# A hybrid DeltaNet and attention block on one core: decay rows in three shared buffers, their exponents on ACT, the first modulation pairs ahead of the norm

## The chip, the cores and the metric

The kernel runs on one core of a Trainium2 chip. The metric is the device time of one execution in microseconds (us), lower is better. The engines are PE (matmuls, with weight loads shown as PEld), DVE (vector), ACT (scalar and activations), POOL (GpSimd) and SP (which issues DMAs). Each engine runs its instructions in the order of its own queue, and an instruction that waits holds up all that stand behind it on that engine.

## The reference

Two layers over 256 context and 256 latent tokens of width 2048. Layer 0 is a gated DeltaNet in chunks, run forward and backward; layer 1 is differential attention. Ahead of each layer the tokens are normed and modulated by shift and scale rows that come from `c` through `ada_w`. The part that the change touches most is the decay inside a chunk, cut to its core:

```python
gc = jnp.cumsum(chunks(g), axis=-1)
diff = gc[..., :, None] - gc[..., None, :]
decay = jnp.where(incl, jnp.exp(jnp.where(incl, diff, 0.0)), 0.0)
kb = kc * bc[..., None]
lower = jnp.where(strict, jnp.einsum('nbhid,nbhjd->nbhij', kb, kc) * decay, 0.0)
tinv = lax.linalg.triangular_solve(eye + lower, ...)
a_intra = jnp.einsum('nbhid,nbhjd->nbhij', qc, kc) * decay
```

## The kernel before

All 512 tokens stand along the free dimension, 128 channels of a head on the partitions. The program is written in Python; a scheduler with a timeline model of its own sorts the instructions of each engine, so that the order on an engine is not that of the code. The head of the program (`body`, lines 296 to 330) loads the tokens `xt`, sums their squares into `acc0`, makes the norm row `rrow0` with two matmuls into `iv`, and computes shift and scale pair by pair: `ada_load` brings the modulation weights `ar` on SP's queue, `ada_pair` multiplies them on PE into the PSUM banks `gq` or `tr` and puts the result into `shv` and `scv`. `make_h` then forms the modulated tokens `hhi` and `hlo` (a value and its rest), which three early projections `ba`, `k0`, `q0` use. `gates` makes the gate rows: the cumulated log decay goes to DRAM as `gc_d` and stays in SBUF as `gct` (with the log of beta taken in), `lnb` holds the limit.

The DeltaNet stage runs over 16 groups `g` of two heads, each with 4 chunks of 128 tokens and both directions. A small event loop (`Drive`) with written priorities sets the order in which the generators are written down: `stream_b` (the recurrence: tiles `yb`, `x`, `S`, `O`, with PSUM `sb` and `so`), `stream_lev` (the levels of the triangular inverse: `T`, `U`, `R`, `uf`, with PSUM `iv`), `stream_at` and `stream_m` (the matrices `at` and `ma`, with PSUM `gq`), `stream_ada` (later modulation, POOL and ACT in turn on `rp`), and `filler` (the projections of the next groups, PSUM `pj`: weights are loaded as raw pieces, cast to `hi` on ACT, the rest `lo` taken on POOL, three buffers each, six matmuls for each piece of 256 columns).

For each chunk, `stream_m` and `stream_at` call `decay` once: 64 times for tiles named `grm` and 64 times for `gra`. It loads four rows of `gc_d`, each copied to all 128 partitions, with two DMAs on SP's queue; makes four DVE instructions of 128x128 that subtract `gct` and take the minimum with `lnb`; and one ACT exponential over 128x512. `scaled` then multiplies the result with the masked Gram matrix `gm` on DVE (line 700) into `ma` or `at`, which frees the buffer. Each of the two tags has one buffer (line 683):

```python
gr = dl.tile([P, 4, P], F32, tag=tag, name=f"{tag}{g}{c}", bufs=1)
```

`block_inv` inverts the 16x16 blocks with a chain of small DVE products (`bP`, `bY`), casts the result into `TU` and stores it to DRAM (`tu_d`), from where `stream_lev` loads `T` and `U` on SP's queue. After the stage the output projections (`woA`, `woB`) and layer 1 follow; their tiles `yr`, `yl` and `woA0r` already appear at the end of the DeltaNet stage.

Of the kernel before, what the change touches and what calls it, by code (L numbers as in the profile page):

```python
# [10 lines left out]
F32 = mybir.dt.float32  # L11
F32R = mybir.dt.float32r
F16 = mybir.dt.float16
BF16 = mybir.dt.bfloat16
AF = mybir.ActivationFunctionType
ALU = mybir.AluOpType
# [4 lines left out]
P = 128  # L21
T = 512
NCH = 4
# [38 lines left out]
def body(ctx, tc, D, d, out):  # L62
    nc = tc.nc
    KT = D // P
    G = KT
    HV = 2 * KT
# [97 lines left out]
    def ada_load(l, pr, pl, tag, bufs):  # L164
        W = 8 * P
        for q in range(2 * D // W):
            r = pl.tile([P, W], F32, tag=tag, name=f"ar{l}_{pr}{q}", bufs=bufs)
            o = q * W % D
            nc.sync.dma_start(r, d["adaw"][l, 2 * pr + q * W // D, :, o:o + W])
            for k in range(W // 256):  # L170
                yield r[:, k * 256:(k + 1) * 256]

    def ada_pair(l, pr, rs, ps, pl):
        for kt, r in enumerate(rs):
            j = 32 * (kt % 4)
            mm(ps[j:j + 32, :256], sc2[:, kt, :], r, kt < 4, kt >= KT - 4)
        row = pl.tile([P, 256], F32, tag="arow", name=f"arow{l}_{pr}", bufs=1)
        nc.scalar.copy(row, ps[:, :256])
        for hf in range(2):
            mm(ps[:, 256 + 2 * hf:258 + 2 * hf], row[:, hf * P:(hf + 1) * P], sel4)  # L180
        for hf in range(2):
            ada_put(l, 2 * pr + hf, ps[:, 256 + 2 * hf:258 + 2 * hf], True)
# [67 lines left out]
    tr = lambda: pt_("tr", 1)  # L250
    iv = lambda: pt_("iv", 2)
# [7 lines left out]

    gp_cm = pool("gp", side="right")  # L260
    gp = gp_cm.__enter__()
    gct, eg, kd, egl, lnb = (gp.tile([P, NCH, 2, HV], F32, name=n) for n in ("gct", "eg", "kd", "egl", "lnb"))
    zt = gp.tile([P, P], F16, name="zt")
    nc.vector.memset(zt, 0.0)
    t0_cm = pool("t0", reuse_waits="tile")
# [1 line left out]
    HKT = KT // 2  # L267
# [27 lines left out]
    ta = ta_cm.__enter__()  # L295
    with tc.high_priority():
        for kt in range(KT):
            nc.sync.dma_start(xt[kt], d["xT"][:, kt])
        nc.scalar.activation(acc0, xt[0], AF.Square)
        for kt in range(1, KT):  # L300
            sq = ta.tile([P, T], F32, tag="mh", name=f"sq{kt}", bufs=2)
            nc.scalar.activation(sq, xt[kt], AF.Square)
            nc.vector.tensor_tensor(acc0, acc0, sq, ALU.add)
        nc.scalar.copy(rrow0, rstd_rows(acc0, T, iv, ta.tile([P, 4, P], F32, name="rr_dg0")))
        np_ = 0
        for k0 in range(0, KT, SK):
            for kind in range(2):
                pr = kind * HKT + k0 // 2
                ada_pair(0, pr, ada_load(0, pr, ta, "ar", 8), (gq, tr)[np_ % 2](), ta)
                np_ += 1  # L310
            for kt in range(k0, k0 + 2):
                make_h((xt[kt][:, 0:256], xt[kt][:, 256:512]), kt, rrow0, 0, hhi, hl, ta, nc.gpsimd)
            for n, src, _ in EARLY:
                w = SK * P
                r = ta.tile([P, w], F32, tag="er", name=f"e{n}r{k0}", bufs=6)
                nc.sync.dma_start(r, src[:, k0 * P:k0 * P + w])
                hi = ta.tile([P, w], F32R, tag="eh", name=f"e{n}h{k0}", bufs=6)
                lo = ta.tile([P, w], F32R, tag="el", name=f"e{n}l{k0}", bufs=6)
                split(hi, lo, r)
                for k in range(SK):  # L320
                    kt, ks = k0 + k, slice(k * P, (k + 1) * P)
                    ps = early[n]
                    mm(ps, hi[:, ks], hhi[:, kt, :], kt == 0, False)
                    mm(ps, hi[:, ks], hl(kt), False, False)
                    mm(ps, lo[:, ks], hhi[:, kt, :], False, kt == KT - 1)
        ta_cm.__exit__(None, None, None)
        convw = load_small("convw", [P, 4 * KT, 5], d["convw"], gp)
        adt = load_small("adt", [P, 2, 2, HV],
                         d["adt"].to_broadcast([P, NB]).rearrange("p (k d h) -> p k d h", k=2, d=2), gp)
# [31 lines left out]
    def gates(ps):  # L361
# [46 lines left out]
        def softplus(k):  # L408
            t, e, u, w = t2[k], tl(f"e{k}", sh), tl(f"u{k}", sh), tl(f"w{k}", sh)
            nc.scalar.activation(e, t, AF.Abs)  # L410
            nc.scalar.activation(e, e, AF.Exp, scale=-1.0)
            nc.vector.tensor_scalar(u, e, 2.0, None, ALU.add)
            nc.vector.reciprocal(w, u)
            nc.vector.tensor_tensor(u, e, w, ALU.mult)
            nc.vector.tensor_tensor(e, u, u, ALU.mult)
            nc.vector.tensor_scalar(w, e, 2.0 / 17.0, None, ALU.mult)
            for m in (15, 13, 11, 9, 7, 5, 3):
                nc.vector.scalar_tensor_tensor(fl(w), fl(w), 2.0 / m, fl(e), ALU.add, ALU.mult)
            nc.vector.scalar_tensor_tensor(fl(w), fl(w), 2.0, fl(u), ALU.add, ALU.mult)
            nc.vector.scalar_tensor_tensor(fl(w), fl(t), 0.0, fl(w), ALU.max, ALU.add)  # L420
            return w
# [3 lines left out]
        nc.vector.tensor_tensor(g, w, wide(ea), ALU.mult)  # L425
        tri = lambda dd: cs[:, C_TRI + dd * P:C_TRI + (dd + 1) * P]
        for a in range(2):
            p3 = (gq, tr)[a]()
            for c in range(2):
                for dd in range(2):  # L430
                    q = 2 * c + dd
                    mm(p3[:HV, q * P:(q + 1) * P], g[:, 2 * a + c, dd, :], tri(dd))
            r = tl(f"r{a}", [HV, 4, P])
            nc.scalar.copy(r.rearrange("p q i -> p (q i)"), p3[:HV])
            nc.sync.dma_start(gc_d[2 * a:2 * a + 2].rearrange("c (d h) i -> h (c d) i", d=2), r)
# [4 lines left out]
                mm(p1v[:, c, dd, :], tri(dd), g[:, c, dd, :])  # L440
        mm(p1[:, n:2 * n], ones, fl(g))
        nc.vector.tensor_scalar(t2[0], bt, -1.0, None, ALU.mult)
        nc.vector.tensor_scalar(lnb, softplus(0), -1.0, None, ALU.mult)
        tc.keep_in_program_order(nc.scalar.activation(eg, p1v, AF.Exp))
        tc.keep_in_program_order(nc.scalar.dma_start(sc_d.rearrange("s (p i) -> (s p) i", i=W2), rc))
        nc.scalar.activation(egl, p1[:, n:2 * n].rearrange("p (c d h) -> p c d h", c=NCH, d=2), AF.Exp)
        raw = tl("raw", sh)
        nc.vector.tensor_copy(raw, p1v)
        nc.vector.tensor_tensor(gct, raw, lnb, ALU.subtract)
        e = tl("be", sh)  # L450
        nc.scalar.activation(e, bt, AF.Exp, scale=-1.0)
        nc.vector.tensor_scalar(e, e, 1.0, None, ALU.add)
# [227 lines left out]
        return t.rearrange("p (u i) -> p u i", u=4)  # L680

    def decay(g, c, s, tag):
        gr = dl.tile([P, 4, P], F32, tag=tag, name=f"{tag}{g}{c}", bufs=1)
        gsrc = gc_d[c].rearrange("(d h) i -> d h i", d=2)
        for dd in range(2):
            nc.sync.dma_start(gr[:, 2 * dd:2 * dd + 2, :],
                              gsrc[dd:dd + 1, 2 * g:2 * g + 2, :].rearrange("d h i -> d (h i)").to_broadcast([P, 2 * P])
                              .rearrange("p (h i) -> p h i", h=2))
        for u in range(4):
            dd, h = divmod(u, 2)  # L690
            j = 2 * g + h
            nc.vector.tensor_scalar(gr[:, u], gr[:, u], gct[:, c, dd, j:j + 1], lnb[:, c, dd, j:j + 1],  # L692
                                    ALU.subtract, ALU.min)
        nc.scalar.activation(gr, gr, AF.Exp)  # L694
        return gr

    def scaled(o, gr, pg, s, nm):
# [5 lines left out]
    def block_inv(g, half, m16):  # L703
        par = half
        nm = f"{g}{half}"
        nc.scalar.dma_start(full(mb_d[par]), m16.rearrange("p d c h i -> p (d c h) i"))
        bk = dl.tile([64, 16, 16], F16, tag="bk", name=f"bk{nm}", bufs=1)
        nc.sync.dma_start(bk, diag(mb_d[par]))
        X = dl.tile([64, 16, 16], F32, tag="bX", name=f"bX{nm}", bufs=1)
        Y = dl.tile([64, 16, 16], F32, tag="bY", name=f"bY{nm}", bufs=1)  # L710
        pr = dl.tile([64, 16, 16], F32, tag="bP", name=f"bP{nm}", bufs=1)
        TU = dl.tile([64, 2, 16, 16], F16, tag="bT", name=f"bT{nm}", bufs=1)
        nc.vector.tensor_scalar(X[:32], bk[:32].rearrange("p j i -> p i j"), -1.0, None, ALU.mult)
        nc.vector.tensor_scalar(X[32:], bk[32:], -1.0, None, ALU.mult)
        nc.scalar.copy(Y, e16[:64])  # L715
        for i in range(1, 16):
            nc.vector.tensor_tensor(pr[:, :i, :i], X[:, i, :i].unsqueeze(1).to_broadcast([64, i, i]),  # L717
                                    Y[:, :i, :i].rearrange("p j c -> p c j"), ALU.mult)
            nc.vector.tensor_reduce(Y[:, i, :i], pr[:, :i, :i], AX.X, ALU.add)  # L719
        for dd in range(2):  # L720
            ps_ = slice(32 * dd, 32 * dd + 32)
            nc.scalar.copy(TU[ps_, dd], Y[ps_])
            nc.scalar.copy(TU[ps_, 1 - dd], Y[ps_].rearrange("p j i -> p i j"))
        for j in range(2):
            nc.scalar.dma_start(diag(tu_d[par][j]), TU[:, j])
        return [tu_d[par][j].rearrange("(d c h) (j i) -> c j d h i", d=2, c=2, i=P) for j in range(2)]
# [574 lines left out]
```

## Time and profile before

| | us |
|---|---|
| median of 3 runs (3129.51 to 3135.29) | 3134.51 |
| the profiled execution | 3130.73 |
| its span, first to last instruction | 3128.9 |
| PE busy (90% of the span) | 2817.8 |
| POOL busy (64%) | 2012.8 |
| DVE busy (63%) | 1955.8 |
| ACT busy (60%) | 1872.4 |

The mean granted clock of PE over the span is 0.963. The busy shares are means over stages of different kinds: head (to some 140 us), the start of the DeltaNet stage (to 300 us), its steady part (to 2000 us), output projections and layer 1. So they are read by stretch, then by who waits for whom within a stretch. Durations come from the profiled execution; 1.8 us of its time lie outside the span.

### The profile page before, as it was taken

To read this page: it belongs to the slowest core of one execution; us is meant where nothing else is said; L and a number is where in the kernel's file an instruction comes from. 1 tells how busy PE (TensorE), PEld (TensorE's weight loads), DVE (VectorE), ACT (ScalarE), POOL (GpSimd) and SP (SyncE) were. 2 spreads that over 40 slices of the span, in tenths; PEclk is the share of its full clock that TensorE was granted. 3 is DMA by queue.
4 is the path that set the end of the run, shared out by engine and by line. 5 is a ranking of instruction groups with operands and counts; after the bars stand their busy time and mean duration, and the time that the engine had idled before them with its cause. 6 is when DMAs were issued, how large, how long until landed. Compare 5 with 4: busy or idle time off the path is not lost. (4 is left out here: it accounts for less than half of the span.)

```text
span 3128.9 us, 52162 instructions
## 1 busy us (share of the span) xinstructions
PE 2817.8 (90%) x16178; PEld 2239.7 (72%) x16178; DVE 1955.8 (63%) x4287; ACT 1872.4 (60%) x5466; POOL 2012.8 (64%) x2370
## 2 busy tenths in 40 slices
PE   5788988988988988988898888899998999999998
PEld 2465767766766766766776666688687888888897
DVE  2178688688678677688578678632335654544454
ACT  4345766766766666766666666654556666654353
POOL 2366777777767777777777777466565666752334
PEclk8899999999999999999999999999999999999999
DMA  9646555456545545445456445667744555543345
GB/s 339 235 100 139 124 127 130 127 119 135 126 118 133 134 116 139 117 125 139 117 126 137 121 120 138 173 178 207 238 147 120 162 155 162 160 142 109 115 130 164
DMA packets 510312, 457.03 MB, mean 146 GB/s; under 512 B 241744, under 2 KB 380752, under 8 KB 510032
## 3 DMA queue, kind: packets, MB, share of 16 engines
q1 hardware_dynamic: 299456, 342.48, 37.7%
q10 hardware_dynamic: 210576, 111.22, 14.9%
q8 instruction: 127, 2.08, 0.3%
q14 instruction: 153, 1.25, 0.1%
HBM read 427.18 MB, written 26.36 MB: 145 GB/s over the span
## 5 line engine op out<-in xcount | busy, mean ns | idle before, releaser
L139 ACT ACTIVATE rp<-rp 128x256 f32<-128x256 f32 x1024 | 426.8, 417 | 298.2 <-POOL rp L138 292.6
L717 DVE TENSOR_TENSOR bP<-bX,bY 64x1 f32<-64x1 f32 (+14 forms) x480 | 225.1, 469 | 22.0 <-ACT bY L715 14.2
L139 ACT ACTIVATION_READ_ACCUMULATOR rp<-rp 128x1 f32 x1024 | 194.2, 190 | 0.0
L692 DVE TENSOR_SCALAR grm<-grm,gct,lnb 128x128 f32<-128x128 f32 x256 | 133.2, 563 | 84.8 <-DMA grm<-gc_d 84.1
L692 DVE TENSOR_SCALAR gra<-gra,gct,lnb 128x128 f32<-128x128 f32 x256 | 116.0, 493 | 85.0 <-DMA gra<-gc_d 84.7
L786 DVE TENSOR_TENSOR R<-iv,lv 128x512 f16<-128x512 f32 x192 | 127.1, 680 | 28.7 <-PE iv L83 28.5
L83 PEld LDWEIGHTS <-m 128*128 128x128 f16 x1024 | 76.2, 100 | 78.7 <-issue 71.5
L694 ACT ACTIVATE grm<-grm 128x512 f32<-128x512 f32 x64 | 40.3, 630 | 129.1 <-DVE grm L692 125.3
L719 DVE TENSOR_REDUCE bY<-bP 64x1 f32<-64x1 f32 (+14 forms) x480 | 108.6, 226 | 8.0
L750 POOL TENSOR_TENSOR ma<-ma,cs 128x512 f32<-128x512 f32 x64 | 86.5, 1352 | 32.3 <-DVE ma L700 30.0
L83 PE MATMUL iv<-T,m 128*128 128x128 f16 x768 | 74.3, 225 | 32.5 <-DMA T<-tu_d 19.1
L83 PE MATMUL iv<-U,R 128*128 128x128 f16 x768 | 76.9, 227 | 28.5 <-DVE R L786 26.4
L694 ACT ACTIVATE gra<-gra 128x512 f32<-128x512 f32 x64 | 40.4, 631 | 103.8 <-DVE gra L692 103.7
L83 PEld LDWEIGHTS <-R 128*128 128x128 f16 x768 | 48.8, 101 | 70.9 <-DVE R L786 37.9
L224 DVE TENSOR_TENSOR hlo<-mh,hhi 128x512 fp32r<-128x512 f32 x32 | 25.9, 833 | 114.9 <-ACT hhi L223 87.8
L83 PE MATMUL sb<-yb,uf 128*128 128x128 bf16 x512 | 55.5, 225 | 32.5 <-DVE yb L910 20.9
L803 ACT CAST T<-iv 128x512 f16<-128x512 f32 x128 | 74.1, 579 | 16.2 <-PE iv L83 12.5
L753 POOL TENSOR_TENSOR ml<-ma,m 128x512 bf16<-128x512 f32 x64 | 75.3, 1177 | 6.2 <-ACT m L752 5.3
L83 PEld LDWEIGHTS <-uf 128*128 128x128 f16 x512 | 36.2, 100 | 57.3 <-issue 52.1
L804 ACT CAST U<-iv 128x512 f16<-128x512 f32 x128 | 75.9, 593 | 0.0
L83 PE MATMUL so<-x,at 128*128 128x128 f32 x512 | 73.3, 280 | 0.3 <-DVE sz L966 0.3
L83 PEld LDWEIGHTS so<-x,at 128*128 128x128 f32 x512 | 67.2, 195 | 2.6 <-PE sb L83 0.4
(2767 smaller groups left out, 11393.0 us busy)
## 6 DMA issues: line engine op xcount, KB each, us to landing
aw<-in_adaw_dram ACTq DMA_DIRECT2D x512, 128.0 KB, 2.9
ar<-in_adaw_dram SPq DMA_DIRECT2D x64, 512.0 KB, 7.5
grm<-gc_d SPq DMA_DIRECT2D x128, 128.0 KB, 4.4
gra<-gc_d SPq DMA_DIRECT2D x128, 128.0 KB, 4.5
mb_d<-m ACTq DMA_DIRECT2D x32, 256.0 KB, 4.9
U<-tu_d SPq DMA_DIRECT2D x128, 64.0 KB, 2.9
T<-tu_d SPq DMA_DIRECT2D x128, 64.0 KB, 3.3
yd<-sz SPq DMA_DIRECT2D x32, 256.0 KB, 3.7
```

Source lines behind the costliest of these rows:

```text
L83: nc.tensor.matmul(o, l, r, start=start, stop=stop)
L139: nc.scalar.activation(pr, pr, AF.Copy, accum_out=acc[:, s, q:q + 1])
L224: nc.vector.tensor_tensor(hlo(kt), t, hhi[:, kt, :].bitcast(F32), ALU.subtract)
L692: nc.vector.tensor_scalar(gr[:, u], gr[:, u], gct[:, c, dd, j:j + 1], lnb[:, c, dd, j:j + 1], ALU.subtract, ALU.min)
L694: nc.scalar.activation(gr, gr, AF.Exp)
L717: nc.vector.tensor_tensor(pr[:, :i, :i], X[:, i, :i].unsqueeze(1).to_broadcast([64, i, i]), Y[:, :i, :i].rearrange("p j c -> p c j"), ALU. ...
L719: nc.vector.tensor_reduce(Y[:, i, :i], pr[:, :i, :i], AX.X, ALU.add)
L750: nc.gpsimd.tensor_tensor(ma, ma, ident.unsqueeze(1).to_broadcast([P, 4, P]), ALU.add)
L753: nc.gpsimd.tensor_tensor(ml[:, :, k], mv, m16[:, :, k], ALU.subtract)
L786: nc.vector.tensor_tensor(R, quad(pp), lvb(n), ALU.mult)
L803: nc.scalar.copy(Tm, quad(pt))
L804: nc.scalar.copy(U, quad(pu))
```

## The change

Four things are changed.

In the head, the loads of `xt` go in turn to SP's and ACT's queues; the two modulation pairs 0 and 8 (`HKT`) are written ahead of the norm and taken out of the loop's first turn.

`decay` has one tag of three buffers for `grm` and `gra`. The four DVE instructions become four ACT activations, Relu of (`gct` - row), and the exponential takes the negative of that; the limit is then zero and no longer `lnb`. `gates` keeps the softplus itself and adds it, so `lnb` falls away.

`TU` takes the buffer of `bP`. In `gates` the second transposed row block goes to `iv` in place of `tr`.

```diff
-    gct, eg, kd, egl, lnb = (gp.tile([P, NCH, 2, HV], F32, name=n) for n in ("gct", "eg", "kd", "egl", "lnb"))
+    gct, eg, kd, egl = (gp.tile([P, NCH, 2, HV], F32, name=n) for n in ("gct", "eg", "kd", "egl"))
...
         for kt in range(KT):
-            nc.sync.dma_start(xt[kt], d["xT"][:, kt])
+            (nc.sync, nc.scalar)[kt % 2].dma_start(xt[kt], d["xT"][:, kt])
+        for pr in (0, HKT):
+            ada_pair(0, pr, ada_load(0, pr, ta, "ar", 8), (gq, tr)[pr > 0](), ta)
         nc.scalar.activation(acc0, xt[0], AF.Square)
...
-            for kind in range(2):
+            for kind in range(2 if k0 else 0):
...
-            p3 = (gq, tr)[a]()
+            p3 = (gq, iv)[a]()
...
-        nc.vector.tensor_scalar(lnb, softplus(0), -1.0, None, ALU.mult)
+        nlnb = softplus(0)
...
-        nc.vector.tensor_tensor(gct, raw, lnb, ALU.subtract)
+        nc.vector.tensor_tensor(gct, raw, nlnb, ALU.add)
...
     def decay(g, c, s, tag):
-        gr = dl.tile([P, 4, P], F32, tag=tag, name=f"{tag}{g}{c}", bufs=1)
+        gr = dl.tile([P, 4, P], F32, tag="gr", name=f"{tag}{g}{c}", bufs=3)
...
-            nc.vector.tensor_scalar(gr[:, u], gr[:, u], gct[:, c, dd, j:j + 1], lnb[:, c, dd, j:j + 1],
-                                    ALU.subtract, ALU.min)
-        nc.scalar.activation(gr, gr, AF.Exp)
+            nc.scalar.activation(gr[:, u], gr[:, u], AF.Relu, scale=-1.0, bias=gct[:, c, dd, j:j + 1])
+        nc.scalar.activation(gr, gr, AF.Exp, scale=-1.0)
...
-        TU = dl.tile([64, 2, 16, 16], F16, tag="bT", name=f"bT{nm}", bufs=1)
+        TU = dl.tile([64, 2, 16, 16], F16, tag="bP", name=f"bT{nm}", bufs=1)
```

The scheduler sorts the engines anew. Three places show it.

SP's queue before, at the last two decays of the stage (`yr` and `woA0r` belong to the output projection; "x2" is two DMAs of one tile):

```order
L686 DMA gra_24410<-gc_d 128x256 x2
L119 DMA yr_24657<-yd 128x512
L119 DMA yr_24666<-yd 128x512
L119 DMA yr_24675<-yd 128x512
L119 DMA woA0r_24684<-in_wout_dram 128x512
L119 DMA yr_24690<-yd 128x512
L686 DMA gra_24422<-gc_d 128x256 x2
```

SP's queue after, at the same two decays (`g15z0r` and `g15z1r` are raw weights of the last projections):

```order
L778 DMA U_23485<-tu_d_89 128x2x128 x2
L778 DMA T_23484<-tu_d_88 128x2x128 x2
L778 DMA T_23490<-tu_d_88 128x2x128 x2
L778 DMA U_23491<-tu_d_89 128x2x128 x2
L119 DMA g15z0r_23819<-in_win_dram 128x512
L688 DMA gra_24408<-gc_d 128x256 x2
L688 DMA gra_24420<-gc_d 128x256 x2
L119 DMA g15z1r_23863<-in_win_dram 128x512
```

The two loads now stand next to each other, ahead of the last raw weights, and behind four loads of `U` and `T`.

DVE before, from the masked Gram matrix of that first decay to its product `at` (`yl` and `woA0lo` belong to the output projection):

```order
L699 TENSOR_TENSOR gm_24419<-gq,cs 128x256
L187 TENSOR_TENSOR yl_24636<-yr_24633,yh_24635 128x512
L187 TENSOR_TENSOR woA0lo_24645<-woA0r_24642,woA0hi_24644 128x512
L692 TENSOR_SCALAR gra_24410<-gra_24410,gct,lnb 128x128 x4
L910 TENSOR_TENSOR yb_24281<-v_23633,sb 128x512
L786 TENSOR_TENSOR R_24120<-iv,lv 128x512
L786 TENSOR_TENSOR R_24127<-iv,lv 128x512
L187 TENSOR_TENSOR yl_24651<-yr_24648,yh_24650 128x512
L187 TENSOR_TENSOR yl_24660<-yr_24657,yh_24659 128x512
L916 TENSOR_TENSOR x_24288<-x_24270,sb 128x512
L700 TENSOR_TENSOR at_24418<-gra_24410,gm_24419 128x512
```

DVE after, the same piece:

```order
L700 TENSOR_TENSOR gm_24417<-gq,cs 128x256
L187 TENSOR_TENSOR yl_24592<-yr_24589,yh_24591 128x512
L143 TENSOR_REDUCE am_16_26307<-al_16_26023 128x2
L911 TENSOR_TENSOR yb_24279<-v_23631,sb 128x512
L701 TENSOR_TENSOR at_24416<-gra_24408,gm_24417 128x512
```

ACT after, where the rows are now made (`g15z0hi` is a cast of a weight piece):

```order
L694 ACTIVATE gra_24408<-gra_24408,gct 128x128 x2
L185 CAST g15z0hi_23762<-g15z0r_23715 128x256
L694 ACTIVATE gra_24408<-gra_24408,gct 128x128 x2
L694 ACTIVATE gra_24420<-gra_24420,gct 128x128 x4
L904 CAST x_23732<-sb 128x512
L185 CAST g15z0hi_23774<-g15z0r_23772 128x256
L139 ACTIVATE rp_17_51_26218,al_17_26024<-rp_17_51_26218 128x256
L135 DMA aw_19_5_26229<-in_adaw_dram 128x256
L695 ACTIVATE gra_24408<-gra_24408 128x512
```

The four row instructions no longer stand ahead of `yb` and `R` on DVE; on ACT eight of them for two decays stand ahead of the cast `x` and the casts of weight pieces.

PE before, its first rows (`iv` from `cs` and `acc` sums the norm over channels, `iv` from `rr_dg` spreads it):

```order
L83 MATMUL iv<-cs,acc_130 128x1 x4
L83 MATMUL gq<-ar_00_228,sc_113 32x256 x4
L83 MATMUL gq<-ar_01_234,sc_113 32x256 x4
L83 MATMUL gq<-ar_02_240,sc_113 32x256 x4
L83 MATMUL iv<-rr_dg_213,cs 128x512
L83 MATMUL gq<-ar_03_246,sc_113 32x256 x4
```

PE after, its first rows:

```order
L83 MATMUL gq<-ar_00_167,sc_112 32x256 x4
L83 MATMUL gq<-ar_01_173,sc_112 32x256 x4
L83 MATMUL iv<-cs,acc_129 128x1 x4
L83 MATMUL gq<-ar_02_179,sc_112 32x256 x4
L83 MATMUL gq<-ar_03_185,sc_112 32x256 x4
L83 MATMUL tr<-ar_80_198,sc_112 32x256 x4
L83 MATMUL iv<-rr_dg_274,cs 128x512
```

Two groups of modulation matmuls moved ahead of the norm's first, and three ahead of its second.

## Rows read from the trace of the kernel before

**Rows 1.** Busy us of each engine by stretch, PE clock, DMA share, GB/s.

```profile
300.00:2000.00 1700.00, 1516.82 (x8975) 1179.18 (x8974) 1273.23 (x2978) 1123.44 (x3450) 1240.82 (x1546) 0.96 0.52 128
...
140.00:300.00 160.00, 126.18 (x567) 94.37 (x568) 122.09 (x252) 79.09 (x227) 95.02 (x113) 0.90 0.45 106
```

**Rows 2.** Waits of PE, 300 to 2000 us: total, times, longest, in us.

```profile
PE iv L83 <- DVE R L786: 26.5, 24, 3.3
PE sb L83 <- DVE yb L910: 18.2, 16, 3.3
...
PE iv L83 <- ACT T L803: 11.9, 12, 3.2
PE sb L83 <- ACT yb L884: 11.4, 10, 2.3
PE gq L83 <- DVE gm L699: 10.7, 8, 3.3
PE sb L83 <- DVE S L923: 9.5, 4, 3.8
PE sb L83 <- ACT x L903: 6.3, 7, 2.5
...
PE pj L83 <- ACT g4z0hi L185: 3.6, 1, 3.6
...
PE pj L83 <- ACT g9z0hi L185: 1.0, 1, 1.0
```

**Rows 3.** DVE's groups, 300 to 2000 us: busy, mean ns, idle before, releasers.

```profile
L786 DVE TENSOR_TENSOR R<-iv,lv 128x512 f16<-128x512 f32 x182 | 120.4, 680 | 27.0 <-PE iv L83 26.8
L692 DVE TENSOR_SCALAR grm<-grm,gct,lnb 128x128 f32<-128x128 f32 x220 | 113.9, 561 | 74.5 <-DMA grm<-gc_d 73.9
L692 DVE TENSOR_SCALAR gra<-gra,gct,lnb 128x128 f32<-128x128 f32 x235 | 106.9, 495 | 79.7 <-DMA gra<-gc_d 79.4
...
L699 DVE TENSOR_TENSOR gm<-gq,cs 128x256 f32<-128x256 f32 x115 | 47.6, 414 | 2.2 <-PE gq L83 1.0
```

**Rows 4.** Waits of SP's DMA queue, 300 to 2000 us.

```profile
SPq L686 <- DVE at L700: 91.5, 38, 6.2
...
SPq L686 <- DVE ma L700: 64.2, 27, 4.9
SPq L777 <- DMA tu_d<-bT: 58.3, 18, 9.9
```

**Rows 5.** Timeline of DVE near 1995 us: start, length, instruction, [idle before].

```profile
1991.75 0.69 DVE L700 TENSOR_TENSOR at<-gra,gm 128x512 f32<-128x512 f32 x1 [0.31 <-PE so L83]
...
1998.19 0.60 DVE L692 TENSOR_SCALAR gra<-gra,gct,lnb 128x128 f32<-128x128 f32 x2 [1.73 <-DMA gra<-gc_d]
```

**Rows 6.** Timeline of SP in the same stretch.

```profile
1992.47 0.80 SPq L686 DMA_DIRECT2D gra<-gc_d  x2
```

**Rows 7.** ACT's groups, 300 to 2000 us.

```profile
L958 ACT ACTIVATE O<-O,f 128x128 f32<-128x128 f32 x116 | 37.3, 392 | 14.7 <-DVE f L955 14.5
L694 ACT ACTIVATE gra<-gra 128x512 f32<-128x512 f32 x58 | 36.6, 632 | 97.1 <-DVE gra L692 97.0
...
L694 ACT ACTIVATE grm<-grm 128x512 f32<-128x512 f32 x55 | 34.6, 630 | 110.7 <-DVE grm L692 106.9 <-DVE bY L719 3.8
```

**Rows 8.** The page's DMA issues: count, KB each, us to landing.

```profile
gra<-gc_d SPq DMA_DIRECT2D x128, 128.0 KB, 4.5
```

**Rows 9.** Busy times by stretch in the head, as in rows 1.

```profile
0.00:5.00 5.00, 0.00 (x0) 0.00 (x0) 0.64 (x3) 1.68 (x2) 0.20 (x4) 1.00 0.59 168
...
15.00:20.00 5.00, 0.00 (x0) 0.00 (x0) 3.49 (x6) 3.90 (x7) 0.00 (x0) 1.00 0.66 210
```

**Rows 10.** Timeline of SP in the head.

```profile
18.67 4.30 SPq L169 DMA_DIRECT2D ar<-in_adaw_dram  x8
```

**Rows 11.** Waits of PE, 20 to 320 us.

```profile
PE iv L83 <- DVE R L786: 3.8, 2, 2.6
PE gq L83 <- DVE gm L699: 3.4, 3, 1.6
```

**Rows 12.** The chain that ended last: start, length, a run of 23 projection matmuls.

```profile
2043.58 5.42 PE pj L83 x23
```

## The prediction

> **What bounds the kernel now.** I read the busy times by stretch first, then who waits in the long middle stretch, then the queues behind those waits. The DeltaNet stage fills 300 to 2000 us of a span of 3128.9 us [rows 1]. There PE is busy 1516.8 of 1700 us; DVE follows with 1273.2, POOL with 1240.8 and ACT with 1123.4. PE's work there is the same before and after, so what a change can win is PE's idle time, 183.2 us, and what the clock loses: a granted clock of 0.96 costs (1 - 0.96) x 1700 = 68 us, 0.37 us per us of idle (my estimate, from these two figures).
>
> PE's idle time is made of many short waits [rows 2]. The four largest on DVE are R 26.5, yb 18.2, gm 10.7 and S 9.5, together 64.9 us in 52 waits. On ACT stand T 11.9, yb 11.4, x 6.3 and the "hi" casts of the weight pieces: eleven rows of 1 us and more, from g4z0hi 3.6 to g9z0hi 1.0, in all 22.6. So the question is what stands ahead of these instructions in DVE's and ACT's queues, since both run in order.
>
> Ahead of them stand the decay rows. DVE spends 113.9 + 106.9 = 221 us on 455 row instructions, and is idle 73.9 + 79.4 = 153 us just before them because the rows have not landed [rows 3]. So the rows hold 374 of DVE's 1700 us. ACT then sits idle 97.0 + 106.9 = 204 us for the same rows, in front of their exponential [rows 7]. The cause is one buffer per kind: SP waits 91.5 and 64.2 us for the products `at` and `ma` before it may load the next rows [rows 4]. One turn of the loop, late in the stage: the product at 1991.75 us, the load issued at 1992.47, and DVE idle for 1.73 us before the row instruction at 1998.19 [rows 5, 6].
>
> **The change part by part.**
>
> Work that leaves DVE: 455 row instructions, 221 us, in this stretch. Occupied time, busy or blocked on rows, is now 1273.2 + 153 = 1426 us (84%); without both it is 1273.2 - 221 = 1052 us (62%).
>
> Work that comes to ACT: as many Relus of 128x128. The nearest row is L958, also 128x128 in SBUF with a per-partition operand: 392 ns as a duration, 37.3 / 116 = 322 ns as a pitch [rows 7]. That makes 455 x 0.322 = 146 to 455 x 0.392 = 178 us; I take 162, the middle, since the order sets the Relus in twos and fours, which overlap in part.
>
> The Trainium skill, page "ScalarE: Activation LUTs", section "Rules for kernel authors", speaks against this: relu, min and add belong on VectorE and not on ScalarE. The rows shown here don't bear that out for this form, since DVE's 561 and 495 ns stand against 392; what the rule would make of the time is the second rival.
>
> The wait on rows moves with them: ACT now waits for the landing, between 0 and DVE's 153 us. In the order after, the two loads of a half stand back to back on SP, where before a product stood between them. So the second decay of each pair finds its rows there, which is half of the waits; and the first gets its buffer from an earlier product than now. I take a third, 50 us.
>
> ACT's occupied time is then 1123.4 + 162 + 50 = 1335 us, against 1123.4 + 204 = 1327 us now: ACT gives back its own waiting for DVE and takes about as much work. I cost it at nothing. The cover for that is those 204 us; without it ACT's waiters would pay (second rival).
>
> What PE gains from the freer DVE: of each wait I keep the waited-for instruction's own time and count only the rest as queueing. R: 26.5 - 24 x 0.68 = 10.2. yb, of the same 128x512 size: 18.2 - 16 x 0.68 = 7.3. gm: 10.7 - 8 x 0.414 = 7.4. S: 9.5 - 4 x 0.68 = 6.8 [rows 2, 3]. Sum **32 us**. The bounds are 0, if DVE still arrives just as late, and 65, if these waits go as a whole. I take the queueing part, since DVE's occupied share falls by 22 points but the products' own times stay.
>
> Clock: 32 x 0.37 = **12 us**.
>
> Start, 140 to 300 us: DVE is busy 122 of 160 us, PE 126 [rows 1]. The same reckoning on R 3.8 (2 waits) and gm 3.4 (3 waits) [rows 11] gives 2.4 + 2.2, so **5 us**; bounds 0 and 7.
>
> Head: the first modulation weights are issued at 18.67 us, behind all loads of x and seven small ones [rows 10]; in the order after the first follows the last x load directly, and two of its matmul groups stand ahead of the norm's. The DMA engines are at 0.59 share in the first 5 us and at 0.66 from 15 to 20 us [rows 9], free for 2.1 + 1.7 = 3.8 us; later stretches up to 130 us are nearly full, so what is sent earlier is gained at the end of the head. The second queue for half of the x loads can fill the first gap, not surely. I take **3 us**, bounds 0 and 3.8. Eight x loads now stand on ACT; ACT waits for the same x there anyway.
>
> Taken at nothing: `lnb` falls away as one DVE instruction; the bank swap of `p3` frees the transposes' bank once; `TU` in the buffer of `bP` makes the next block's first product wait for the store of the last one, but a block comes only every 53 us (32 in 1700).
>
> Sum: 32 + 12 + 5 + 3 = **52 us**. Against the profiled execution of 3130.7 us that is 3079; the median of the runs shown is 3134.5, 4 us above it, so I say **3081 us**.
>
> **The rivals.**
>
> More than the queueing part goes (the order after also puts other matmuls where PE now sits through a product's own time): all 65 us, so 33 x 1.37 = 45 more, about **3036 us**. For it: DVE gives back time in each of the 128 decays. Against it: these chains run product by product, and a product keeps its 0.68 us.
>
> ACT takes over as the engine that is late. Its occupied time at the upper bounds is 1123.4 + 178 + 153 = 1454 us (86%, from 78%); its free share falls from 22 to 14%. PE's 52 us of waits on ACT (11.9 + 11.4 + 6.3 + 22.6) then grow by 22/14, by 30 us, with the clock 41: about **3122 us**. This is what the rule of the Trainium skill named above ("ScalarE: Activation LUTs", "Rules for kernel authors") would come to here. For it: the casts T and U, yb, x and all "hi" casts stand in this one queue. Against it: the 204 us that ACT no longer waits for DVE.
>
> The third buffer changes little (both kinds now share it, and a row set that waits for its product keeps it from the other kind): DVE loses its instructions, ACT waits for rows as DVE did. I give half of the 32, with the clock 22, and 8 for start and head, less 10 for ACT: 3131 - 20, about **3111 us**.
>
> Slower: the row loads are stuck in SP's queue. In the order after, the last pair stands behind four loads of U and T, and such a load waits for its store, 58.3 us in 18 times, 9.9 at the longest [rows 4]. ACT at the Relu then blocks the "hi" casts. PE has three cast pieces of six matmuls in hand, 18 x 5.42 / 23 = 4.2 us [rows 12]; that is the point from which it decides. A landing of 4.5 us [rows 8] and a mean wait of 58.3 / 18 = 3.2 leave 7.7 - 4.2 = 3.5 us of bare PE. In one decay of each of the 32 halves that is 112 us: 3081 + 112 = **3193 us**. From some 17 such decays on the kernel is slower than before. For it: that piece of the order. Against it: such a wait delays SP's row loads before, too, and the longest wait of PE on a cast is 3.6 us.
>
> **How the numbers follow.** Forecast 3081 (own range 3050 to 3110): 0.55. More, 3036: 0.15. ACT late, 3122: 0.15. Buffer of little use, 3111: 0.07. Slower by stuck rows, 3193: 0.08. What a measurement of this kernel can tell from no change is about 0.2%, 6 us, so 3128 to 3141. Half of the case "ACT late" lies above 3122: I give 0.05 of it to "same" and 0.02 to "slower", and 0.02 of the forecast to "same". Faster 0.83, same 0.07, slower 0.10. The range 3030 to 3128 leaves out the slower case, the upper part of "ACT late" and the lowest part of "more", together nearly 0.2.
>
> **What would show it.** Right: DVE's occupied time in the stretch near 1050 us, its waits on rows gone, ACT's wait for rows near 50 us and its busy time near 1285, SP's wait for `at` and `ma` far below 156 us, PE's waits on R, yb, gm and S near half, a clock of 0.97. A row instruction on ACT shows 0.39 us. Head: the first matmul before 20 us and the end of full DMA some 3 us earlier. Wrong: PE's waits on T, yb and the casts up by more than those on DVE fall; ACT's wait for rows above 150 us; single waits of PE on a cast above 4 us; or Relus well over 0.4 us.

## The result, and the profile after

The changed kernel takes 3079.11 us (median of 4 runs, 3072.65 to 3084.25) beside 3134.53 us for the kernel before on the same chip: a ratio of 0.9825, 95% interval 0.9801 to 0.985. The forecast was 3081. The profiled execution took 3072.65 us, 58.1 less than before; its span is 3070.9 us.

Because the stage now ends earlier, a fixed window of 300 to 2000 us holds different work in the two kernels. From here on "the stage" is the same part of the work in each (some instructions cross its edges, so the counts differ by up to 1%): from the first copy of `S` on DVE to the first tile `xb` of the output projection. Busy us of each engine (PE, weight loads, DVE, ACT, POOL, with instructions), then PE's clock, DMA share and GB/s, before:

```profile
318.30:2020.30 1702.00, 1515.19 (x8954) 1176.69 (x8954) 1274.96 (x2978) 1126.24 (x3456) 1235.56 (x1539) 0.96 0.52 128
```

and after:

```profile
313.00:1958.50 1645.50, 1504.96 (x9004) 1157.24 (x9003) 1097.83 (x2514) 1233.87 (x3825) 1202.26 (x1497) 0.98 0.53 131
```

The stage is 56.5 us shorter. PE's idle time in it falls from 186.8 to 140.5 us, 46.3 less; the other 10.2 are PE's busy time, at a granted clock of 0.98 in place of 0.96. Outside the stage the head gives 2.9, the start 2.4 and the first part of the output projection 1.5 us, and the rest of the program takes 5.3 back (926.6 to 931.9 us): 56.5 + 2.9 + 2.4 + 1.5 - 5.3 = 58.0, the change of the span.

What PE waits for in the stage after (total, times, longest):

```profile
PE iv L83 <- DMA T<-tu_d: 14.5, 11, 3.5
PE iv L83 <- DVE R L787: 12.9, 16, 2.1
PE sb L83 <- ACT yb L885: 8.8, 7, 4.1
PE sb L83 <- DVE S L924: 6.7, 5, 2.7
PE sb L83 <- ACT x L904: 5.5, 4, 3.6
PE pj L83 <- ACT g10khi L185: 5.1, 3, 3.0
PE pj L83 <- ACT g3v0hi L185: 4.0, 1, 4.0
...
PE iv L83 <- ACT T L804: 3.7, 8, 1.1
PE gq L83 <- DVE gm L700: 3.2, 3, 2.7
PE sb L83 <- DVE yb L911: 3.1, 4, 1.7
```

R, yb, gm and S stood at 26.5, 18.2, 10.7 and 9.5 in [rows 2]; they now come to 25.9 together. (Within the stage before, yb and S were 20.9 and 10.8.) Summed over all rows of this view, PE's waits on DVE fall from 87.1 to 37.1 us, those on ACT stay (61.1 and 59.7), those on DMA stay (15.2 and 15.7), and those on POOL rise from 18.8 to 22.9.

The row instructions on ACT, in the place of DVE's in [rows 3] (busy, mean ns, idle before):

```profile
L694 ACT ACTIVATE gra<-gra,gct 128x128 f32<-128x128 f32 x232 | 81.5, 395 | 87.6 <-DMA gra<-gc_d 84.7 <-DVE bY L720 2.2 <-DVE x L917 0.3
L694 ACT ACTIVATE grm<-grm,gct 128x128 f32<-128x128 f32 x224 | 78.0, 394 | 60.3 <-DMA grm<-gc_d 59.0 <-DVE bP L718 0.9
```

The wait for rows has not gone. DVE lost 156 us of it in this stage before; ACT now loses 84.7 + 59.0 = 143.7 in the same way. And SP still waits for the products before it may load, 138 us for 156 before [rows 4] (all waits of the row loads together fall from 234 to 180 us):

```profile
SPq L709 <- DMA mb_d<-m: 90.7, 25, 5.8
SPq L688 <- DVE ma L701: 81.8, 29, 8.5
SPq L688 <- DVE at L701: 56.5, 34, 5.4
SPq L778 <- DMA tu_d<-bT: 49.6, 16, 5.9
```

### The profile page after: what moved, and what is told of

It is laid out like the page before. It is cut to its first block, busy times and chain, and to the rows that moved or that the text cites. A ratio compares the mean times of both kernels' runs of the same rounds, so it can differ in the third digit from the quotient of the medians.

```text
span 3070.9 us, 52214 instructions
## 1 busy us (share of the span) xinstructions
PE 2802.3 (91%) x16178; PEld 2215.8 (72%) x16178; DVE 1763.3 (57%) x3774; ACT 2011.7 (66%) x5978; POOL 2017.8 (66%) x2370
## 5 line engine op out<-in xcount | busy, mean ns | idle before, releaser
L694 ACT ACTIVATE gra<-gra,gct 128x128 f32<-128x128 f32 x256 | 89.8, 395 | 92.5 <-DMA gra<-gc_d 89.6
L694 ACT ACTIVATE grm<-grm,gct 128x128 f32<-128x128 f32 x256 | 88.7, 394 | 69.3 <-DMA grm<-gc_d 67.8
L701 DVE TENSOR_TENSOR ma<-grm,gm 128x512 f32<-128x512 f32 x64 | 54.6, 853 | 51.5 <-POOL ml L754 35.2
L871 POOL TENSOR_TENSOR kx<-ktok,kd 128x256 f32<-128x256 f32 x96 | 63.4, 681 | 9.2 <-PE sb L83 6.6
L880 DVE SCALAR_TENSOR_TENSOR y<-sb,eg,v 128x128 f32<-128x128 f32 x192 | 54.2, 338 | 23.3 <-PE sb L83 23.3
L700 DVE TENSOR_TENSOR gm<-gq,cs 128x256 f32<-128x256 f32 x128 | 53.2, 416 | 25.0 <-PE gq L83 23.4
```

Of the source, the lines that this page charges most:

```text
L694: nc.scalar.activation(gr[:, u], gr[:, u], AF.Relu, scale=-1.0, bias=gct[:, c, dd, j:j + 1])
L871: nc.gpsimd.tensor_tensor(kx[:, dd], ktok[:, cd[dd]].unsqueeze(1).to_broadcast([P, 2, P]), kd[:, cd[dd], dd, 2 * g:2 * g + 2].unsqueeze(2) ...
```

## The experiments

**The question.** Theory: the gain is the 456 row instructions that leave DVE, since PE then finds R, yb, gm and S done; ACT takes them at no cost. Rivals: the third buffer, the head, or `TU`'s buffer brings it; or ACT's wait for rows has a price that some other part hides. The runs below stood in three rounds (e, f and g), each on another chip and beside the kernel before, which took 3121.0 to 3121.5 us there. One table holds them all, with the ratio to the kernel before of the same round; the last three columns are of each kernel's own stage, in us: PE's waits on DVE, PE's waits on ACT, and the wait for rows of the engine that makes the row instructions. The first two lines were traced in the first measurement, where the kernel before took 3134.5 us, so their stage lengths don't compare with those below. The changed kernel and f0 are the same program: two traces of it differ by 5 us in PE's waits on ACT and by 10 us in the wait for rows.

| kernel | ratio | 95% interval | stage | PE on DVE | PE on ACT | rows |
|---|---|---|---|---|---|---|
| before | 1 | | 1702.0 | 87.1 | 61.1 | DVE 156 |
| changed | 0.9825 | 0.9801-0.985 | 1645.5 | 37.1 | 59.7 | ACT 144 |
| f0_changed_again | 0.9809 | 0.9781-0.9837 | 1642.9 | 37.5 | 54.5 | ACT 134 |
| e1_exp_on_dve | 1.0107 | 1.0084-1.013 | 1722.3 | 93.3 | 55.4 | DVE 147 |
| e2_one_buffer_each | 0.9814 | 0.9793-0.9834 | 1648.6 | 30.7 | 53.6 | ACT 139 |
| e3_old_head | 0.9829 | 0.9803-0.9854 | 1640.5 | 37.4 | 51.4 | ACT 132 |
| e4_head_only | 0.9993 | 0.9981-1.0006 | 1689.7 | 85.0 | 57.0 | DVE 143 |
| f1_move_only | 0.9901 | 0.9876-0.9925 | 1664.2 | 35.7 | 73.7 | ACT 169 |
| f2_dve_one_each_tu_own | 1.0032 | 1.0019-1.0045 | 1717.5 | 95.1 | 56.3 | DVE 155 |
| f3_dve_one_each_tu_shared | 0.9991 | 0.9979-1.0003 | 1697.2 | 87.3 | 64.2 | DVE 143 |
| g1_tu_own | 0.9943 | 0.9919-0.9968 | 1691.1 | 45.7 | 75.3 | ACT 192 |
| g2_old_bank | 0.9896 | 0.9865-0.9927 | 1665.3 | 45.6 | 69.1 | ACT 175 |
| g3_act_gra_only | 0.9962 | 0.9946-0.9977 | 1681.0 | 60.9 | 66.4 | both 177 |
| g4_one_load | 1.0015 | 0.9998-1.0031 | 1711.6 | 37.8 | 101.8 | ACT 212 |

**The exponents back on DVE, the rest of the change kept.**

```diff
-            nc.scalar.activation(gr[:, u], gr[:, u], AF.Relu, scale=-1.0, bias=gct[:, c, dd, j:j + 1])
-        nc.scalar.activation(gr, gr, AF.Exp, scale=-1.0)
+            nc.vector.tensor_scalar(gr[:, u], gr[:, u], gct[:, c, dd, j:j + 1], 0.0, ALU.subtract, ALU.min)
+        nc.scalar.activation(gr, gr, AF.Exp)
```

> The changed kernel with one part undone: the decay exponents and their limit are made by four DVE instructions again (row minus gct, minimum with zero), all else as changed, the three shared buffers too. Theory 'work moved': the gain of the DeltaNet stage (56 us between the first copy of S and the first output projection) comes from taking 221 us of instructions and 153 us of waiting for rows off DVE; then most of it is lost here, 3115 to 3130 us, and DVE again sits idle for rows by 100 us or more. Theory 'buffers': it comes from rows that land earlier; then it stays near 3085 to 3095 us and DVE's wait for rows is well below 153 us.

Measured 1.0107, a larger loss than theory 'work moved' had: without the move the rest of the change costs time. PE's waits of that stage:

```profile
PE iv L83 <- DVE R L787: 26.3, 33, 3.2
PE sb L83 <- DVE yb L911: 20.8, 18, 3.0
PE iv L83 <- DMA T<-tu_d: 20.5, 13, 3.7
PE sb L83 <- DVE x L917: 12.5, 9, 3.9
...
PE gq L83 <- DVE gm L700: 9.9, 9, 2.1
```

R, yb and gm stand where they stood in [rows 2]. The row instructions on DVE are what brings them back.

**One buffer for each kind of row, the rest of the change kept.**

```diff
-        gr = dl.tile([P, 4, P], F32, tag="gr", name=f"{tag}{g}{c}", bufs=3)
+        gr = dl.tile([P, 4, P], F32, tag=tag, name=f"{tag}{g}{c}", bufs=1)
```

> The changed kernel with one part undone: grm and gra have one buffer each again, in place of three shared ones; the exponents stay on ACT. Theory 'work moved': within 10 us of the changed kernel, 3075 to 3090 us, with ACT's wait for rows near the 144 us that it has with three buffers. Theory 'buffers': 3105 to 3130 us, with ACT's wait for rows above 200 us and PE's waits on casts up with it.

Measured 0.9814, no different from the changed kernel (0.9825, and 0.9809 when run again), with 139 us of waiting for rows in place of 134 to 144. Whatever the three shared buffers bring, nothing of it is left in the time.

**The head, taken out and alone.** e3 is the changed kernel with the old loads of `xt` and the old place of the two pairs; e4 the kernel before with the new ones.

```diff
-            (nc.sync, nc.scalar)[kt % 2].dma_start(xt[kt], d["xT"][:, kt])
-        for pr in (0, HKT):
-            ada_pair(0, pr, ada_load(0, pr, ta, "ar", 8), (gq, tr)[pr > 0](), ta)
+            nc.sync.dma_start(xt[kt], d["xT"][:, kt])
...
-            for kind in range(2 if k0 else 0):
+            for kind in range(2):
```

> The changed kernel with one part undone: the head as before (all loads of x on SP's queue, no modulation pair ahead of the norm). If the head is worth its 3 us by itself: 3082 us, the copy of the gate rows (gt_baT) at 150 us in place of 147, and the stage after it as long as in the changed kernel. Rival 'order': every edit makes the scheduler lay out the whole program anew, and this alone moves the time by 10 us or more; then the time differs from 3082 by that much, with the head's part still 3 us.

> The kernel before with the new head alone. Head worth 3 us: 3131 us, gt_baT at 147 us. Rival 'order': another layout of the stage moves the time by 10 us or more either way, with the head's part still 3 us.

Measured 0.9829 without it and 0.9993 with it alone: 0 to 0.2%, not told apart from nothing. PE does start earlier in the changed kernel (start, length, the idle time before it):

```profile
19.04 1.08 PE L83 MATMUL gq<-ar,sc 128*32 128x256 f32 x8 [19.04 <-DVE acc L305]
```

where the kernel before had its first modulation matmuls at 23.68. But the head's last gate copy comes at 148.8 to 149.9 us in the three kernels with the old head and at 145.8 to 150.7 in the eleven with the new one, so the 2.9 us between the first two traces lie within what the layout alone moves. Of the two gaps that the forecast named in the DMA engines' work, the one from 15 to 20 us is filled (share 0.66 before, 1.03 after), the one in the first 5 us is not (0.59 and 0.57).

**The changed kernel again, and the move alone.** f1 is the kernel before with the Relus and the exponential of the change and `lnb` dropped, nothing else.

> The changed kernel itself, beside the three below on one chip. Ratio to the kernel before 0.9825, as measured.

> The kernel before with one part of the change alone: the exponents and their limit on ACT. One buffer for each of grm and gra, TU in its own buffer, old head, old bank of the gate rows. Theory 'work moved': the whole gain, a ratio of 0.980 to 0.985, with DVE's occupied time in the stage down and ACT's wait for rows near 145 us, as in the kernels with one and with three buffers. Rival 'the parts need each other': the move alone gives less than half, a ratio above 0.991, since ACT now waits for each row set behind its own last product.

The move alone gives 0.9901, half of the gain: more than the rival allowed and less than the theory. PE's waits on DVE are as low as in the changed kernel (35.7), but those on ACT are 19 us above it in the same company (73.7 and 54.5), and ACT's wait for rows is 169 us.

**The exponents on DVE with one buffer each, `TU` in its own buffer (f2) or in that of `bP` (f3).** Both have the edit of e1 and that of e2; f2 also has

```diff
-        TU = dl.tile([64, 2, 16, 16], F16, tag="bP", name=f"bT{nm}", bufs=1)
+        TU = dl.tile([64, 2, 16, 16], F16, tag="bT", name=f"bT{nm}", bufs=1)
```

> The changed kernel with its exponents back on DVE, one buffer for each of grm and gra, and TU in a buffer of its own: of the change the head, the bank of the gate rows and the dropped lnb are left. The kernel with exponents on DVE and three buffers came to 1.0107 of the kernel before. If the shared buffers are what costs there, this one is at 0.997 to 1.001. Rival 'dropped lnb and new bank lay the stage out worse': it stays at 1.008 or more.

> As the one before, but with TU in the buffer of bP, as in the change. If the wait of DVE's block products for the store of TU (24.6 us in the kernel with three buffers) is what costs, this one is slower than the one before by 15 to 30 us, a ratio near 1.006; if the three shared row buffers are, it is within 5 us of it.

1.0032 and 0.9991: f2 lies between its two theories, and f3 is 12 us faster than f2 where its theories had it slower or equal. f3 differs from e2 only in the engine that makes the row instructions, so the move is worth 0.9991 - 0.9814 = 1.8% there. The kernel that shares `TU`'s buffer is 0.4% faster, not slower. And e1 against f3, three shared buffers against one each, costs 1.2% with the exponents on DVE. Why is not settled: the largest difference in PE's waits is on DMA (20.5 us in e1, 7.3 in f3), and the orders differ throughout.

**What lies between 0.990 and 0.981.** g1 is e2 with f2's edit; g2 is e2 with the old bank in `gates`:

```diff
-            p3 = (gq, iv)[a]()
+            p3 = (gq, tr)[a]()
```

> The changed kernel with one buffer for each kind of row (which measured 0.981 of the kernel before) and TU in a buffer of its own again. Between that kernel and the one that only moves the exponents (0.990) lie three edits: TU's buffer, the bank of the second transposed row block, the head. Theory A, TU's buffer is worth what it was worth with the exponents on DVE (0.9991 against 1.0032, 0.4%): 0.985, with PE's wait for the hi casts up from some 36 to some 40 us. Theory B, TU's buffer alone carries the rest of the gain: 0.989 to 0.990. Theory C, it is worth nothing and the gap is in the bank or the head: 0.981 to 0.982.

> The changed kernel with one buffer for each kind of row and the second transposed row block in its old bank. Theory A, the bank is used once, before the stage, and is worth nothing by itself: 0.980 to 0.983. Theory B, the scheduler's whole order hangs on it, as on any small edit: a shift of up to 0.5% with the busy times of all engines and the count of loads unchanged, and the stage's length, not the start, takes it.

0.9943 and 0.9896: all three theories on g1 missed, and the bank, used once ahead of the stage, moves the time by 0.8%, more than theory B allowed. It has no work in the stage that could cost 17 us. What it changes is the scheduler's order: place by place, 8,416 of PE's 16,178 matmuls in the trace are others than in e2. g1 has old and new edits together and is slower than f1, which has more of the old ones. So small edits aren't additive here; each brings another order, and kernels one such edit apart differ by up to 1.3%. The move itself can be compared in four pairs that differ in little else: before and f1 gain 1.0%, f2 and g1 0.9%, f3 and e2 1.8%, e1 and the changed kernel 2.8%. It gains in all four, but how much depends on the order around it. No kernel here beats the changed one by more than the intervals.

**Half of the move.** g3 is e2 with the exponents of `gra` on ACT and those of `grm` on DVE.

```diff
-            nc.scalar.activation(gr[:, u], gr[:, u], AF.Relu, scale=-1.0, bias=gct[:, c, dd, j:j + 1])
-        nc.scalar.activation(gr, gr, AF.Exp, scale=-1.0)
+            if tag == "gra":
+                nc.scalar.activation(gr[:, u], gr[:, u], AF.Relu, scale=-1.0, bias=gct[:, c, dd, j:j + 1])
+            else:
+                nc.vector.tensor_scalar(gr[:, u], gr[:, u], gct[:, c, dd, j:j + 1], 0.0, ALU.subtract, ALU.min)
+        nc.scalar.activation(gr, gr, AF.Exp, scale=-1.0 if tag == "gra" else 1.0)
```

> The changed kernel with one buffer for each kind of row; the exponents of gra are made by ACT, those of grm by DVE as before the change. Theory A, the gain follows what DVE is rid of: half of the way between 0.999 (all on DVE) and 0.981 (all on ACT), so 0.990, with PE's waits on DVE near 60 us (87 and 31 at the ends). Theory B, it is DVE's blocking that counts and one kind left on DVE blocks as before: 0.995 or more, PE's waits on DVE 75 us or more. Theory C, the larger part goes with the first kind, since DVE is then no longer full: 0.985 or less, PE's waits on DVE 45 us or less.

PE's waits on DVE are 60.9 us, halfway, as theory A had it to the us. The time, 0.9962, is not halfway but in theory B's range: the waits on ACT are 66.4, 13 above e2. DVE's load sets one kind of wait; the time is set by both.

**One load for a decay.** g4 is e2 with one DMA of 256 KB in place of two of 128.

```diff
-        for dd in range(2):
-            nc.sync.dma_start(gr[:, 2 * dd:2 * dd + 2, :],
-                              gsrc[dd:dd + 1, 2 * g:2 * g + 2, :].rearrange("d h i -> d (h i)").to_broadcast([P, 2 * P])
-                              .rearrange("p (h i) -> p h i", h=2))
+        nc.sync.dma_start(gr.rearrange("p (d h) i -> p d (h i)", d=2),
+                          gsrc[:, 2 * g:2 * g + 2, :].rearrange("d h i -> d (h i)").partition_broadcast(P))
```

> The changed kernel with one buffer for each kind of row, and one DMA for each decay in place of two. ACT waits some 140 us for rows in the stage. Theory A, that wait costs PE nothing, since PE's waits on ACT are no larger than before the change: 0.980 to 0.983 whatever happens to the wait. Theory B, it costs: a wait that falls by a third (fewer issues on SP's queue, 0.4 us each for 128 decays) gives some 5 us, 0.979, and one that grows loses as much.

1.0015: the whole gain is gone. The load lands later (the page's DMA issues: count, KB, us to landing), and no Relu can start on a first half any more,

```profile
grm<-gc_d SPq DMA_DIRECT2D x64, 256.0 KB, 5.0
gra<-gc_d SPq DMA_DIRECT2D x64, 256.0 KB, 5.1
```

against 4.2 and 4.3 in e2, and ACT waits 212 us in the stage:

```profile
ACT grm L692 <- DMA grm<-gc_d: 111.6, 42, 5.6
ACT gra L692 <- DMA gra<-gc_d: 100.5, 46, 6.8
```

PE's waits on DVE stay at 37.8 us; those on ACT rise from 53.6 to 101.8, the "hi" casts alone from 39.4 to 60.7. Theory A falls: ACT's wait for rows is paid by PE. Theory B has the sign right, but its price, some 5 us for 46 us of wait, is far too low. (The order differs from e2's too, so not all of the 2% need be the landing.)

**What the table says together.** Over the 14 lines of the table (13 kernels, one of them twice) the time follows the sum of PE's waits on DVE and on ACT: a straight line through them has 1.1 us of time for 1 us of wait, with a correlation of 0.95. Over the eight lines with all row instructions on ACT it follows ACT's wait for rows: 0.76 us for 1 us, correlation 0.98, from 132 us at 0.9829 to 212 at 1.0015 (0.69 and 0.97 without g4). That is a relation over kernels whose orders differ too; only g4 moved the wait on purpose.

**Where that wait comes from.** One decay of the changed kernel, the longest wait. SP (start, length, instruction, count):

```profile
1288.97 0.59 SPq L709 DMA_DIRECT2D bk<-mb_d  x1
1289.67 1.06 SPq L688 DMA_DIRECT2D gra<-gc_d  x2
```

ACT:

```profile
1293.49 0.40 ACT L694 ACTIVATE gra<-gra,gct 128x128 f32<-128x128 f32 x1 [4.23 <-DMA gra<-gc_d]
1293.80 0.39 ACT L185 CAST g10v0hi<-g10v0r 128x256 fp32r<-128x256 f32 x1
```

PE:

```profile
1294.24 0.50 PE L83 MATMUL pj<-hhi,g10v0hi 128*128 128x512 f32 x1 [1.36 <-ACT g10v0hi L185]
```

The rows are loaded right behind `bk`, which waits for the store of `mb_d` (90.7 us in 25 times, above); ACT stands 4.23 us at the Relu; the cast queued behind it comes late, and PE waits 1.36 us for that cast. In the five longest waits of ACT for `gra` (4.23, 3.29, 3.22, 3.20 and 2.89 us) the rows follow a load of `bk` four times (SP had waited 3.7, 5.8, 4.5 and 1.1 us for its store) and once a raw weight piece behind loads of `T`. Those are the tail; most of the 119 waits are short, 1.2 us in the mean. Counted from the trace by what SP waited for last before it issued the load (if that ended less than 1.5 us before), most of the 143.7 us is still the row load's own wait for DVE: 91 us in 84 waits, 62 of it for the products `at` and `ma`. A store of `mb_d` ahead of the load stands behind 21 us in 10 waits, a raw weight piece that waited for POOL behind 17 in 15. In e2, with one buffer each, the same three are 104, 4 and 24 us: the changed kernel has 13 us less of waiting for DVE, but 17 us more of waiting behind `bk`. `block_inv` issues the store of `mb_d` from ACT's own queue, so a late ACT can delay the very rows that it waits for; how much that costs wasn't tested. Loading the rows from another queue wasn't tried.

## Why the prediction came out right

**Bound and cause: right.** DVE's queue was the largest part of what PE waited for, 87 of 182 us. All eight lines of the table with all row instructions on ACT have 31 to 46 us of PE's waits on DVE, all five with all on DVE 85 to 95, and the one in between 60.9. It is not the whole cause: g4 keeps these waits at 37.8 and has lost the gain on ACT's side.

**DVE's load: the size was off.** Forecast was 1052 us of occupied time in 300 to 2000; the stretch after shows more work:

```profile
300.00:2000.00 1700.00, 1559.46 (x9289) 1201.02 (x9289) 1126.19 (x2575) 1266.30 (x3928) 1240.68 (x1545) 0.98 0.53 132
```

In the same work DVE's busy time falls by 177 us, not by the 221 of the step. Counts fall by the row instructions (2978 to 2514), so the group's busy time overstates what the engine gets back. By the trace before, the row instructions have DVE to themselves for only 199.8 of their 222 us and overlap a neighbour for the rest; and DVE's other instructions take 22.6 us more than before (1075.2 to 1097.8), for a reason that stays open. A new wait came for it, which the step had taken at nothing:

```profile
L718 DVE TENSOR_TENSOR bP<-bX,bY 64x225 f32<-64x225 f32 (+14 forms) x421 | 199.5, 474 | 31.3 <-DMA tu_d<-bT 19.5 <-ACT rp L139 1.9 <-ACT cyg10v L474 1.5
```

The 19.5 us are the store of `TU` out of `bP`'s buffer. No loss of time by it shows: f3, which has 18.8 us of this wait, is faster than f2, which gives `TU` a buffer of its own.

**PE's waits on DVE: 32 forecast, 50 measured.** In the stage (where yb stood at 20.9 and S at 10.8 before) R gave 13.6 (10.2 forecast), yb 17.8 (7.3), gm 7.5 (7.4) and S 4.1 (6.8), 43 together where the sum had 32, and other tiles 7. Mis-sized was yb: the step kept the instruction's own 0.68 us in each of 16 waits, but 13 of 17 went as a whole; in the stage before it stood at

```profile
PE sb L83 <- DVE yb L910: 20.9, 17, 3.3
```

PE's other idle time grew by 4, so 46 us of the 50 are left.

**Clock: 12 forecast, 10.2 measured.** The price per us of idle was too high (10.2 / 46.3 = 0.22 for 0.37) where the idle time was too low. Neither is firm: f0, the same program, has 1510.6 us of PE's busy time in the stage, 5.7 more than the first trace.

**ACT at nothing: right in the sum, wrong in the reason.** The Relus were forecast at 0.39 us and 162 us; the rows show 395 and 394 ns and 159.5 us. The Trainium skill, page "ScalarE: Activation LUTs", section "Rules for kernel authors", would keep such work on VectorE; the measured 0.9991 against 0.9814 says otherwise for this kernel. The wait for rows, forecast at 50, is 143.7: this is the step that failed. It counted on loads back to back and on the third buffer. SP still waits 138 us for the products, the wait is not longer with one buffer each (139 in e2), and it moved from DVE to ACT with the instruction that has it. PE's waits on ACT stayed level because T gave 8.2 and yb 2.6 us while the "hi" casts took 10.7 more. And the cover of 204 us was not roomy, as "at nothing" says: g4, at 1223 + 212 = 1435 us of ACT's time, has lost it all. That is the second rival, priced at 1454 us of occupied time and 3122; in g4 it is real, and it begins earlier than it was put.

**Start 5, head 3.** Measured 2.4 and 2.9. For the head that shows little: e3 and e4 can't tell it from nothing.

**The other rivals.** "More" (all 65 us of R, yb, gm and S): 43 went, between the two. "Third buffer of little use": true of the buffer, but the rival took half of DVE's gain away for it, and PE's waits on DVE fell by more than forecast. "Slower by stuck rows": the mechanism is there, behind `bk` more often than behind `U` and `T`, but it leaves single waits of PE on a cast of 4.0 us at most, and few.

**Not in the sum: what is given back later.** The rest of the program is 5.3 us longer. The later modulation (`rp`) runs beside the stage; with a shorter stage less of it is done there, and ACT's part from the last `xb` to the end grows from

```profile
L139 ACT ACTIVATE rp<-rp 128x256 f32<-128x256 f32 x295 | 122.8, 416 | 106.2 <-POOL rp L138 105.3 <-DMA xl<-xs_d 0.4
```

to

```profile
L139 ACT ACTIVATE rp<-rp 128x256 f32<-128x256 f32 x347 | 144.5, 416 | 132.2 <-POOL rp L138 131.1 <-issue 0.4
```

That these 52 pieces make the 5.3 us is argued, not shown. So the sum, 52, was 6 us short of the 58 between the two profiled executions (errors of both signs that largely cancel): 14.3 too little of PE's idle time and 1.5 of the output projection that it left out, against 1.8 too much of the clock, 2.7 of start and head, and the 5.3 given back. That 3081 lies within 2 us of the median is partly luck, since the median after stands 6.5 us above its profiled execution.

## What to carry to other kernels

An instruction that waits for a DMA takes its wait along when it moves to another engine: price the move by who stands behind it in each queue, not by busy time alone. Before giving such a load more buffers, look what its queue waits for, because a load stuck behind another gains nothing from a free buffer. Where a scheduler sorts everything, undoing one small edit measures the new order too; believe what separates all variants, not a single difference of about 1%.

## What the hardware showed beside that

The subtract-and-clamp of a 128x128 tile in float32 takes ACT 391 to 395 ns in the kernels that make it there, while DVE took 493 and 563 ns with two operands per partition (means over the whole program) and still 424 to 528 with a constant limit (e1, f2, f3, g3). One load of 256 KB landed 5.0 to 5.1 us after its issue in the median (g4), 0.8 us later than one of 128 KB in e2.
